# Forget gates, softmax scaling and the end of the first projection: three moves in a two-layer encoder kernel

## The chip, the cores and the metric

The kernel runs on one core of one Trainium2 chip. The metric is device time in microseconds of one execution, the median of the runs shown. One further execution was taken with the hardware profiler; all rows quoted here are from its profile and trace.

The engines are PE (TensorE, matmul), DVE (VectorE), ACT (ScalarE), POOL (GpSimd) and SP (SyncE, which issues most of the DMAs). Each takes its instructions from a queue, in order, so an instruction that waits holds up all that stand behind it on the same engine.

## The reference, cut to what matters

A sequence of 512 tokens of width 1024 goes through two layers. Each layer is a half-step SwiGLU, a mixer, and another half-step SwiGLU, each behind an RMSNorm with shift and scale. The change lies in the mixer:

```python
def hybrid_mixer(h, w_in, ...):
    proj = h @ w_in
    qa, ka, va, ub, qc, kc, vc, f_lin, g_lin = jnp.split(proj, SPLIT_POINTS, axis=-1)
    ya = chunked_relpos_attention(ha(qa), ha(ka), ha(va), ...)       # 8 heads of 64, learned bias
    yb = multiscale_pool(ub, w_pool, pool_scale)
    yc = forgetting_attention(hc(qc), hc(kc), hc(vc), ..., f_lin + forget_bias)
    ...
def forgetting_attention(q, k, v, gq, gk, f_logit):
    cum_logf = jnp.cumsum(jax.nn.log_sigmoid(f_logit), axis=1)       # per head, over the sequence
    logits = q k^T + (cq[..., None] - cum_k[:, :, None, :])          # causal
    p = jax.nn.softmax(logits, axis=-1)
    return p @ v
```

Queries and keys are RMS-normalised per head. Attention A is banded with a learned bias, attention C is causal with the forget gates as bias. The three branches are then gated, summed and projected.

## The kernel before

**Arithmetic.** Every large matmul is done as three passes of float32r: high part by high part, high by low, low by high (`triple`, line 117). A weight chunk is loaded by SP into a `raw` buffer (two of them), cast to its high part on ACT (line 268) and subtracted to its low part on DVE (line 270), by `wchunk`. `qkv_chunk` loads two of the eight 128-row blocks of one of the six 512-column projections.

**Order.** The code is unrolled Python, and a scheduler puts the instructions of each engine in order when the kernel is built, by the order in the code and by when it reckons operands to be ready. The code steers with a counter, `pe[0]`, in units of one 512-column pass on PE: a `triple` adds 3. `later(delay, fn)` sets a task due so many passes on; `poll`, called at each `triple`, runs what is due. `gate` and `behind` (lines 231 to 241) tie the weight casts and subtractions that follow a norm behind that norm's last instruction on ACT and DVE.

**The mixer** (`Mixer.run`, line 953):

1. `drain` runs the query, key and value projection of attention A one after the other (`proj_qk` with column block 0 and 1, `proj_v` with 2). A projection holds four accumulators (PSUM tag `acc`, four banks), one for each 128 tokens; `evac` empties them. For a query or key the evacuation is a copy and a square on ACT (lines 651 and 653) and a reduction on DVE (line 654); later tasks work out the norm, scale, and turn the result by transposes on PE (lines 660 to 694).
2. `attention` (line 777) goes through 8 heads of 4 row blocks. Row block i has (i + 1) x 128 columns. `logits` does two matmuls (lines 788, 789), bias and row maximum on DVE (792), Exp with row sum on ACT (796), the reciprocal on DVE (798) and the scaling of the row by it on POOL (799), and asks for `turn` `LAG_T` = 24 passes later. `turn` transposes the row on PE (811) and splits it in two parts on ACT and DVE (815, 816); `weigh`, `LAG_V` = 14 passes later, multiplies with the values (833, 834) and adds the halves (837 to 840). Between row blocks the loop draws products from a `filler` until the counter has gone up by a budget.
3. Attention A's filler is query, key and value projection of attention C and then `forget`, with a budget of `FILL_A` = 9.5. Attention C's filler is the merge of branch A (`merge_units`), with `FILL_C` = 9.0.

`forget` (line 726) does 16 matmuls of 40 output rows by 512 columns into a bank of the PSUM tag `mm`, then a chain of small instructions on 8 partitions: sums on DVE (740, 742), Exp on ACT (743), an addition (744), Ln on ACT (745), a difference (746), the running sum (748), and four differences (754); two DMAs write the result to memory, from where attention C's `strip_c` reads it back, spread over all partitions, as bias of each head. It is the last thing that the filler gives.

**The first projection** is special. Its first three weight chunks were loaded and split before the mixer (`self.pre`; the first two lie in the two buffers of tag `ptb`, one of which the evacuated query needs too), and the norm of the hidden state comes in two halves of 256 tokens. So `proj` (line 594) does six of the eight blocks for the first two token tiles, while the norm of the second half is made on DVE and ACT, then six blocks for the last two tiles. Only then is the fourth chunk asked for, and the last two blocks of all four tiles follow, each tile with its evacuation.

Working tiles that matter: `t1` has two buffers (biased logits, partial outputs), `t2` three (the scaled rows of the softmax from Exp to turn, and the squares of an evacuation).

Of the kernel before, what the change touches and what calls it, by code (L numbers as in the profile page):

```python
# [19 lines left out]
ALU = mybir.AluOpType  # L20
# [11 lines left out]
NT = T // P  # L32
# [8 lines left out]
def encoder_kernel(tc, xT, c, w_ada, b_ada, gains, w_gate, w_up, w_down, w_qkv, w_f, w_ubg,  # L41
                   qk_gain, rel, fbias, w_pool, pool_scale, w_branch, w_out, inv_cnt, w_first, out):
    nc = tc.nc
# [20 lines left out]
    def st(shape, dt, tag, bufs):  # L64
        return sb.tile(shape, dt, tag=tag, bufs=bufs, name=nm(tag))

    def acc(shape=(P, T)):
        return ps.tile(list(shape), F32, tag="acc", bufs=4, name=nm("acc"))

    def mmt(shape=(P, T)):  # L70
        return ps.tile(list(shape), F32, tag="mm", bufs=4, name=nm("mm"))
# [5 lines left out]
    def t1(cols=T):  # L77
        return st([P, cols], F32, "t1", 2)

    def t2(cols=T):  # L80
        return st([P, cols], F32, "t2", 3)
# [16 lines left out]
    def later(delay, fn, group=None):  # L98
        t = Task(pe[0] + delay, fn, group)
        tasks.append(t)  # L100
        return t
# [272 lines left out]
    def split_to(hi, lo, src):  # L374
        nc.scalar.copy(hi, src)
        nc.vector.tensor_tensor(lo, src, hi.bitcast(F32), op=ALU.subtract)
# [213 lines left out]
    def qkv_chunk(l, col, c, **kw):  # L590
        return wchunk(w_qkv[l, 2 * c * P:(2 * c + 2) * P, col * T:(col + 1) * T]
                      .rearrange("(k p) c -> p k c", p=P), (2, T), **kw)

    def proj(l, col, evac, pre=None, norm=None):
        accs = [acc() for _ in range(NT)]

        def three(t, k, hi, lo):
            tk = slice(t * P, (t + 1) * P)
            triple2(accs[t], hhi[:, k, tk], hlo[:, k, tk], hi, lo, k == 0, k == KD - 1)

        if norm is not None:
            for hs in range(2):
                norm.back(hs, mmt)
                if hs == 0:
                    later(FRONT2, lambda: norm.front(1, mmt))
                    later(BACK2, lambda: norm.back(1, mmt))
                for k in range(6):
                    hi, lo = pre[k // 2]
                    for t in (2 * hs, 2 * hs + 1):
                        three(t, k, hi[:, k % 2, :], lo[:, k % 2, :])  # L610
        else:
            for c in range(2):
                hi, lo = qkv_chunk(l, col, c)
                for kk in range(2):
                    for t in range(NT):
                        three(t, 2 * c + kk, hi[:, kk, :], lo[:, kk, :])
                        yield
        held = [(c, *qkv_chunk(l, col, c)) for c in ((3,) if pre else (2, 3))]
        for t in range(NT):
            for c, hi, lo in held:  # L620
                for kk in range(2):
                    three(t, 2 * c + kk, hi[:, kk, :], lo[:, kk, :])
                    yield
            evac(t, accs[t])

    def triple2(o, lh, ll, rh, rl, start, stop):
        triple(o, lh, ll, rh, rl, start, stop)

    def proj_v(l, col, tag, res):
        vt = [None] * NT  # L630

        def evac(t, a):
            b = st([P, H, 2, HD], F32R, tag, 4)
            a3 = a.rearrange("p (h d) -> p h d", h=H)
            for odd in range(2):
                hi, lo = b[:, odd::2, odd, :], b[:, odd::2, 1 - odd, :]
                split_to(hi, lo, a3[:, odd::2, :])
            vt[t] = b

        yield from proj(l, col, evac)  # L640
        res.extend(vt)
# [135 lines left out]
    def attention(qs, ks, vs, strip, ys, filler, budget, group):  # L777


        open_pt = {}  # L780

        def logits(h, i, strips):
            p, off = divmod(h, 2)
            (q, ql), k = qs[p], ks[p]
            odd = h % 2
            n = (i + 1) * P
            s = mmt()
            mm(s[:, :n], q[:, odd, i * P:(i + 1) * P], k[:, odd, :n], start=True, stop=False)
            mm(s[:, :n], ql[:, odd, i * P:(i + 1) * P], k[:, odd, :n], start=False, stop=True)
            lg = t1(T)[:, :n]  # L790
            mx = st([P, 1], F32, "mx", 4)
            nc.vector.tensor_tensor_reduce(out=lg, in0=s[:, :n], in1=strips[i], scale=-1.0, scalar=BIG,
                                           op0=ALU.add, op1=ALU.min, accum_out=mx)
            pr = t2(T)[:, :n]
            sm = st([P, 1], F32, "sm", 4)
            nc.scalar.activation(pr, lg, AF.Exp, bias=mx, scale=-1.0, accum_out=sm)  # L796
            rs = st([P, 1], F32, "rs", 4)
            nc.vector.reciprocal(rs, sm)  # L798
            nc.gpsimd.tensor_scalar(pr, pr, rs, None, op0=ALU.mult)  # L799
            pe[0] += 0.5 * (i + 1.5)  # L800
            later(LAG_T, lambda: turn(h, i, pr), group)

        def turn(h, i, pr):
            half, c = divmod(i, 2)
            nj = 2 * half + 2
            if c == 0:
                open_pt[h] = st([P, 2, nj, 256], F32R, "ptb" if half else "pta", 2 if half else 1)
            pt = open_pt[h]
            tp = mmt()
            for j in range(i + 1):  # L810
                nc.tensor.transpose(tp[:, j * P:(j + 1) * P], pr[:, j * P:(j + 1) * P], ident)  # L811
            tv = tp[:, :(i + 1) * P].rearrange("p (j q) -> p j q", q=P)
            dh = pt[:, 0, :i + 1, c * P:(c + 1) * P]
            dl = pt[:, 1, :i + 1, c * P:(c + 1) * P]
            nc.scalar.copy(dh, tv)
            nc.vector.tensor_tensor(dl, tv, dh.bitcast(F32), op=ALU.subtract)
            pe[0] += 0.55 * (i + 1)
            if c == 1:
                later(LAG_V, lambda: weigh(h, half, pt), group)

        def weigh(h, half, pt):
            p, off = divmod(h, 2)
            rows = slice(off * HD, off * HD + HD)
            other = slice(HD - off * HD, 2 * HD - off * HD)
            if off == 0 and half == 0:
                ys.append(blk("b"))
            y = ys[p]
            o = mmt((P, HALF))
            nj = 2 * half + 2
            for j in range(nj):  # L830
                q0 = P if j == nj - 1 else 0
                v2 = vs[j][:, h, :, :].rearrange("p a d -> p (a d)")
                mm(o[:, q0:], v2, pt[:, 0, j, q0:], start=(j == 0), stop=False)
                mm(o[:, q0:], v2, pt[:, 1, j, q0:], start=False, stop=(j == nj - 1))
            cols = slice(half * HALF, (half + 1) * HALF)
            yl = t1(T)[:, :HALF]
            nc.scalar.copy(yl[rows, :], o[other, :])
            nc.vector.tensor_tensor(yl[rows, :], o[rows, :], yl[rows, :], op=ALU.add)
            nc.scalar.copy(y[rows, 0, cols], yl[rows, :])
            nc.gpsimd.tensor_tensor(y[rows, 1, cols], yl[rows, :], y[rows, 0, cols].bitcast(F32), op=ALU.subtract)  # L840
            pe[0] += 1.0 * nj

        for h in range(H):
            strips = strip(h)
            if group == "c":
                finish_turns(h // 2)
            for i in range(NT):
                logits(h, i, strips)
                if i == NT - 1:
                    heads[0] = h + 1  # L850
                poll()
                goal = pe[0] + budget
                while filler is not None and pe[0] < goal:
                    if next(filler, "end") == "end":
                        filler = None
                poll()
        if filler is not None:
            for _ in filler:
                pass

    LAG_T, LAG_V = 24, 14


    def pool_front(l, g):
# [77 lines left out]
    class Mixer:  # L942
# [10 lines left out]
        def run(self, nxt):  # L953
            l = self.l
            in_ffn[0] = False
            for b in range(4):
                nc.gpsimd.dma_start(x_dram[b], x_blocks[b].rearrange("p a t -> p (a t)"))
            g = qkgc[:, l, :]
            g8 = qg8[:, l, :]
            qa, ka, va, qc, kc, vc = [], [], [], [], [], []  # L960
            ya, yb, yc = [], [], []
            drain(proj_qk(l, 0, g8[:, 0:1], True, qa, self.pre, self.norm),
                  proj_qk(l, 1, g[:, 1:2], False, ka), proj_v(l, 2, "xv", va))
            finish_turns()
            turns.clear()
            heads[0] = 0
# [1 line left out]
            def fill_a():  # L968
                yield from proj_qk(l, 3, g8[:, 2:3], True, qc)
                yield from proj_qk(l, 4, g[:, 3:4], False, kc)  # L970
                yield from proj_v(l, 5, "v2", vc)
                yield from forget(l)

            lo_share[0] = LO_SHARE
            attention(qa, ka, va, lambda h: strip_a(l, h), ya, fill_a(), FILL_A, "a")
# [61 lines left out]
                    d = c0 // P + j  # L1037
                    residual_tail(d, hs, o, modc[:, l, 5, d:d + 1], nxt)

    FILL_A, FILL_C = 9.5, 9.0  # L1040
    LO_SHARE = 0

    phases = []
# [65 lines left out]
```

## Time and profile before

| | |
|---|---|
| median of 3 runs | 2469.67 us (2468.43 to 2471.49) |
| the profiled execution | 2469.75 us |
| its span, first to last instruction | 2467.7 us |
| granted TensorE clock | 0.999 |
| POOL scaling of a row (line 799), all widths | 128 times, 138.4 us |

A page of the profile lists each engine's busy time. A row of the waits gives who waited for whom, the time in total, how often, and the longest. A row of the stages gives the stretch, its length and then for PE, PEld (weight loads of PE), DVE, ACT and POOL the busy time with the number of instructions in brackets, then the granted clock, the DMA share and GB/s. A row of the timeline gives start and duration in us, engine, line, operation, output and inputs, shapes, how many neighbours were merged, and in brackets the idle time before it and what ended it. A matmul is drawn longer than it holds PE: the next one of a run starts before its end.

### The profile page before, as it was taken

Reading aid. Unit: us, or ns where it says so; the run is one execution under the profiler, and the core shown is the slowest. Engines: PE = TensorE matmul, PEld = TensorE weight load, DVE = VectorE, ACT = ScalarE, POOL = GpSimd, SP = SyncE. Lnnn points to the kernel's source line nnn. Section 1 sums busy time; section 2 is a strip of 40 time slices with the busy share of each in tenths; the row PEclk is TensorE's granted clock in tenths of the full one; section 3 lists DMA queues with packets and bytes.
Section 4 is the critical chain, followed back from the end, with each engine's and each line's share of the span. In section 5 each row is a group of like instructions: output and inputs, shape, how many; then the busy total and the mean of one; then the engine's idle time right before and its main releaser. Section 6 shows DMA issues by size and latency. Waiting matters only on the chain.

```text
span 2467.7 us, 31105 instructions
## 1 busy us (share of the span) xinstructions
PE 2420.8 (98%) x11898; PEld 2027.6 (82%) x11898; DVE 1313.8 (53%) x2346; ACT 979.8 (40%) x1634; POOL 399.7 (16%) x455
## 2 busy tenths in 40 slices
PE   7999999998999999999999999999989999999999
PEld 5888888776888898888898888978778888888888
DVE  8655536676543465555365533376765434533332
ACT  5222235676632442223342222366765323422221
POOL 3000011145632200000100000112465322000000
PEclk9999999999999999999999999999999999999999
DMA  7655542223323435565335532323233233223222
GB/s 275 222 196 188 196 136 87 86 73 98 109 94 103 153 102 198 174 208 180 120 118 189 189 118 94 129 90 94 73 99 104 86 120 128 77 94 102 94 94 94
DMA packets 116264, 320.03 MB, mean 130 GB/s; under 512 B 11122, under 2 KB 13298, under 8 KB 116116
## 3 DMA queue, kind: packets, MB, share of 16 engines
q1 hardware_dynamic: 114962, 313.86, 38.3%
q0 software_dynamic: 1152, 4.19, 0.4%
q8 instruction: 93, 1.52, 0.3%
q14 instruction: 55, 0.45, 0.1%
q10 hardware_dynamic: 2, 0.00, 0.0%
HBM read 311.64 MB, written 6.38 MB: 129 GB/s over the span
## 4 chain that ended last, share of the span: by engine, by line
PE 86%; DVE 5%; ACT 5%; POOL 2%; issue 2%; DMA 0%; DVEq 0%; POOLq 0%; ACTq 0%
PE acc L119 14%; PE acc L120 14%; PE acc L121 14%; PE mm L121 14%; PE mm L119 14%; PE mm L120 14%; POOL t L799 1%; PE mm L811 1%; ACT whi L268 1%; ACT b L686 1%; DVE wlo L270 1%; ACT b L689 1%; DVE v L197 1%; POOL b L840 1%; ACT t L796 1%
## 5 line engine op out<-in xcount | busy, mean ns | idle before, releaser
L268 ACT CAST whi<-raw 128x1024 fp32r<-128x1024 f32 (+1 forms) x395 | 411.7, 1045 | 1076.5 <-PE acc L120 411.2
L270 DVE TENSOR_TENSOR wlo<-raw,whi 128x1024 fp32r<-128x1024 f32 x387 | 475.7, 1231 | 532.7 <-ACT whi L268 520.3
L121 PE MATMUL mm<-hhi,wlo 128*128 128x512 f32 x1304 | 507.5, 389 | 0.4 <-DVE wlo L270 0.4
L119 PE MATMUL mm<-hhi,whi 128*128 128x512 f32 x1304 | 507.7, 389 | 0.0
L120 PE MATMUL mm<-hlo,whi 128*128 128x512 f32 x1304 | 507.4, 389 | 0.0
L119 PE MATMUL acc<-b,whi 128*128 128x512 f32 (+1 forms) x960 | 356.0, 371 | 0.0
L120 PE MATMUL acc<-b,whi 128*128 128x512 f32 (+1 forms) x960 | 353.7, 368 | 1.3 <-POOL b L840 1.3
L121 PE MATMUL acc<-b,wlo 128*128 128x512 f32 (+1 forms) x960 | 354.0, 369 | 0.0
L121 PEld LDWEIGHTS mm<-hhi,wlo 128*128 128x128 f32 x1304 | 244.8, 188 | 51.5 <-DVE wlo L270 0.9
L119 PEld LDWEIGHTS mm<-hhi,whi 128*128 128x128 f32 x1304 | 245.1, 188 | 50.8
L120 PEld LDWEIGHTS mm<-hlo,whi 128*128 128x128 f32 x1304 | 244.8, 188 | 50.9
L197 DVE CUSTOM_DVE_ANT_0 v<-v,b,badac 128x1024 f32<-128x1024 f32 x144 | 189.3, 1316 | 34.5 <-DMA v<-in_w_ada_dram 34.4
L120 PEld LDWEIGHTS acc<-b,whi 128*128 128x128 f32 x960 | 181.2, 189 | 30.8 <-POOL b L840 1.9
L121 PEld LDWEIGHTS acc<-b,wlo 128*128 128x128 f32 x960 | 181.1, 189 | 29.8
L119 PEld LDWEIGHTS acc<-b,whi 128*128 128x128 f32 x960 | 181.1, 189 | 28.9
L119 PE MATMUL acc<-hhi,whi 128*128 128x512 f32 x480 | 190.8, 399 | 1.7 <-ACT hhi L563 1.7
L120 PE MATMUL acc<-hlo,whi 128*128 128x512 f32 x480 | 188.3, 392 | 1.1 <-DVE hlo L566 1.1
L121 PE MATMUL acc<-hhi,wlo 128*128 128x512 f32 x480 | 188.0, 392 | 0.0
L799 POOL TENSOR_SCALAR t<-t,rs 128x128 f32<-128x128 f32 (+3 forms) x128 | 138.4, 1084 | 251.1 <-DVE rs L798 220.3
L461 DVE TENSOR_TENSOR t<-mm,t 128x512 f32<-128x512 f32 x86 | 59.4, 691 | 204.7 <-PE mm L121 203.5
L119 PE MATMUL acc<-whi,hhi 128*128 128x512 f32 x336 | 137.9, 411 | 4.0 <-ACT t L653 3.6
L121 PE MATMUL acc<-whi,hlo 128*128 128x512 f32 x336 | 132.1, 393 | 0.0
(232 smaller groups left out, 3346.6 us busy)
## 6 DMA issues: line engine op xcount, KB each, us to landing
v<-in_w_ada_dram SPq DMA_DIRECT2D x144, 512.0 KB, 4.5
raw<-in_w_down_dram SPq DMA_DIRECT2D x88, 512.0 KB, 3.7
raw<-in_w_up_dram SPq DMA_DIRECT2D x82, 512.0 KB, 3.5
raw<-in_w_gate_dram SPq DMA_DIRECT2D x79, 512.0 KB, 3.6
raw<-in_w_ubg_dram SPq DMA_DIRECT2D x56, 512.0 KB, 3.5
raw<-in_w_qkv_dram SPq DMA_DIRECT2D x42, 512.0 KB, 3.8
raw<-in_w_branch_dram SPq DMA_DIRECT2D x24, 512.0 KB, 3.7
raw<-in_w_out_dram SPq DMA_DIRECT2D x16, 512.0 KB, 3.6
```

The lines of the kernel that those rows point to most:

```text
L119: mm(o, lh, rh, start=start, stop=False)
L120: mm(o, lh, rl, start=False, stop=False)
L121: mm(o, ll, rh, start=False, stop=stop)
L197: dot = nc.vector.tensor_tensor_reduce(out=raw, in0=raw, in1=silc[0], scale=1.0, scalar=badac[:, l, j, d:d + 1], op0=ALU.mult, op1=ALU.add ...
L268: nc.scalar.copy(hi, raw)
L270: lo_eng.tensor_tensor(lo, raw, hi.bitcast(F32), op=ALU.subtract)
L461: nc.vector.tensor_tensor(pr, pu, sg, op=ALU.mult)
L686: nc.scalar.activation(dst[own, :], pt[own, :], AF.Identity, scale=gc)
L689: nc.scalar.activation(low, pt[own, :], AF.Identity, scale=gc)
L796: nc.scalar.activation(pr, lg, AF.Exp, bias=mx, scale=-1.0, accum_out=sm)
L799: nc.gpsimd.tensor_scalar(pr, pr, rs, None, op0=ALU.mult)
L811: nc.tensor.transpose(tp[:, j * P:(j + 1) * P], pr[:, j * P:(j + 1) * P], ident)
```

## The change

It has four parts. In `proj`, when a norm is passed, the fourth chunk is asked for as soon as the first half's six blocks are issued, and the last two blocks and the evacuation follow for each half by itself. In `logits`, rows of 512 columns are scaled on VectorE, the others on GpSimd as before. The turn of a row is asked for 30 passes after its logits, in both attentions. `forget` moves from the end of attention A's filler to between the key and the value projection of attention A, and the filler's budget goes from 9.5 to 9.0.

```diff
@@ proj
+                both = (2 * hs, 2 * hs + 1)
                 for k in range(6):
                     hi, lo = pre[k // 2]
-                    for t in (2 * hs, 2 * hs + 1):
+                    for t in both:
                         three(t, k, hi[:, k % 2, :], lo[:, k % 2, :])
+                if hs == 0:
+                    rest = qkv_chunk(l, col, 3)
+                for t in both:
+                    for kk in range(2):
+                        three(t, 6 + kk, rest[0][:, kk, :], rest[1][:, kk, :])
+                    evac(t, accs[t])
+                yield
+            return
         else:
...
-        held = [(c, *qkv_chunk(l, col, c)) for c in ((3,) if pre else (2, 3))]
+        held = [(c, *qkv_chunk(l, col, c)) for c in (2, 3)]
@@ logits
-            nc.gpsimd.tensor_scalar(pr, pr, rs, None, op0=ALU.mult)
+            eng = nc.vector if i == NT - 1 else nc.gpsimd
+            eng.tensor_scalar(pr, pr, rs, None, op0=ALU.mult)
@@
-    LAG_T, LAG_V = 24, 14
+    LAG_T, LAG_V = 30, 14
@@ Mixer.run
             drain(proj_qk(l, 0, g8[:, 0:1], True, qa, self.pre, self.norm),
-                  proj_qk(l, 1, g[:, 1:2], False, ka), proj_v(l, 2, "xv", va))
+                  proj_qk(l, 1, g[:, 1:2], False, ka), forget(l),
+                  proj_v(l, 2, "xv", va))
...
                 yield from proj_v(l, 5, "v2", vc)
-                yield from forget(l)
@@
-    FILL_A, FILL_C = 9.5, 9.0
+    FILL_A, FILL_C = 9.0, 9.0
```

## The prediction

> **What bounds the kernel now.** I read the page first, then who waited for whom on PE, then the busy time of the engines stage by stage, and last the timeline around the few places that were left.
>
> ```profile
> span 2467.7 us, 31105 instructions
> ...
> PE 2420.8 (98%) x11898; PEld 2027.6 (82%) x11898; DVE 1313.8 (53%) x2346; ACT 979.8 (40%) x1634; POOL 399.7 (16%) x455
> ```
>
> TensorE is the bound: 46.9 us of the span are not matmul time. No edit removes a matmul, so all that can move is PE's waiting. The waits of PE, over the whole run:
>
> ```profile
> PE mm L811 <- POOL t L799: 13.2, 18, 1.8
> PE mm L552 <- ACT ssum L548: 4.6, 1, 4.6
> PE mm L539 <- DVE ssum L535: 4.0, 1, 4.0
> PE mm L145 <- ACT b L133: 3.7, 1, 3.7
> PE acc L119 <- ACT t L653: 3.6, 6, 1.3
> PE mm L788 <- DVE mx L792: 3.2, 6, 1.1
> PE mm L788 <- DVE t L838: 3.1, 5, 1.1
> ```
>
> L145, L539 and L552 belong to the start, which the change does not touch. The rest belongs to the mixer: the softmax transposes (L811) wait for the scaling on POOL (L799), projections wait for a bank that is still being evacuated (L653), logits (L788) wait for DVE. By stage, the first layer's mixer and one stage of the second's:
>
> ```profile
> 0.00:33.00 33.00, 19.01 (x56) 12.23 (x57) 25.41 (x45) 18.19 (x29) 10.21 (x12) 1.00 0.81 291
> ...
> 412.00:460.00 48.00, 46.73 (x222) 38.12 (x221) 34.58 (x64) 30.68 (x46) 0.00 (x0) 1.00 0.28 86
> 460.00:560.00 100.00, 95.51 (x500) 77.55 (x500) 72.45 (x187) 71.64 (x158) 42.05 (x50) 1.00 0.25 77
> 560.00:620.00 60.00, 52.37 (x280) 40.37 (x279) 39.92 (x111) 41.22 (x97) 37.98 (x50) 1.00 0.34 109
> 620.00:690.00 70.00, 69.17 (x371) 57.95 (x370) 40.37 (x104) 41.13 (x95) 40.44 (x50) 1.00 0.35 109
> ...
> 1780.00:1840.00 60.00, 52.74 (x278) 41.24 (x276) 39.77 (x110) 40.40 (x95) 37.63 (x49) 0.97 0.35 109
> ```
>
> The first figure after the length is PE's busy time. Idle: 1.3 in the key and value projection, 4.5 in attention A, 7.6 where A turns into C, 0.8 in the steady part of C, 14.2 us in all. The second layer repeats it (7.3 against 7.6 in the costly stage), so both layers hold about 28 us. That is the purse, and over half of it lies in 60 us at the A to C seam.
>
> **The change part by part.** *Forget gates between key and value.* The 16 matmuls are moved, not added. What they cover is this wait on PE:
>
> ```profile
> 435.90 0.39 PE L120 MATMUL acc<-wlo,hhi 128*128 128x512 f32 x1
> 436.13 0.39 PE L121 MATMUL acc<-whi,hlo 128*128 128x512 f32 x1
> 437.79 0.50 PE L119 MATMUL acc<-whi,hhi 128*128 128x512 f32 x1 [1.27 <-ACT t L653]
> ```
>
> Matmuls of 512 columns start every 0.23 us here; the value projection starts 1.66 us after the last one, so the wait costs 1.43, not the 1.27 called idle (0.16 more each time PE stops, since a matmul's end is drawn long). Sixteen matmuls at 0.23 are 3.7 us that need no accumulation bank, so the wait goes: -1.4 per layer, **-2.9** in all.
>
> At their old place the gates' vector steps stand in the queues of attention A:
>
> ```profile
> 565.01 0.73 DVE L740 SCALAR_TENSOR_TENSOR t<-mm,fbc,t 8x512 f32<-8x512 f32 x1
> ...
> 571.85 0.47 DVE L754 TENSOR_SCALAR ssum<-t 8x512 f32<-8x512 f32 x1
> ```
> ```profile
> 572.77 0.50 PE L788 MATMUL mm<-b,b 128*128 128x512 f32 x1 [1.05 <-DVE t L838]
> ...
> 575.28 0.33 PE L788 MATMUL mm<-b,b 128*128 128x128 f32 x1 [1.09 <-DVE mx L792]
> ```
>
> From 565.0 to 572.3 DVE works almost only for the gates, and directly behind them PE stops twice, for an attention output (L838) and a row maximum (L792) that stood in the queue. With 0.16 each that is 2.5 per layer, **-4.9**. At the new place the same 7.3 us of chain run beside the value projection (32 products of three matmuls, 22 us of PE). Queued behind it on DVE are the subtractions that make the value weights' low parts and the key's turning; ACT's table loads for Exp and Ln lie inside the chain; on SP the write of the gate vectors waits for its end, with weight loads behind it; the gates' own load and POOL's memset have nobody waiting. Cover is 3.7 us of new PE work, so the price lies between 0 and 7.3 - 3.7 = 3.6 per layer. The stage waits 1.3 today and DVE is busy 34.6 of 48, so I stay near the low end: 1 per layer, **+2**.
>
> *The pacing of attention A.* Without the gates the filler of A is 3 x 32 products of 3 passes, 288, which is 32 rows at 9.0; before it was 304, 32 rows at 9.5. But a budget of 9.5 is overrun: products come in threes, so a row takes 12 with little turning in it. Following the counter row by row through the code, the old filler is used up at the logits of row 7,0 and the last four rows are issued 6, 1, 1 and 2 passes apart; with 9.0 and no lump of 16 the filler lasts to the last row, which all stand 10 to 19 passes apart. The trace shows the bunch:
>
> ```profile
> 565.15 0.33 PE L788 MATMUL mm<-b,b 128*128 128x128 f32 x1 [0.25 <-DVE mx L792]
> 565.80 0.39 PE L788 MATMUL mm<-b,b 128*128 128x256 f32 x1
> 567.06 0.36 PE L788 MATMUL mm<-b,b 128*128 128x384 f32 x1
> ...
> 586.37 0.91 PE L811 MATMUL mm<-ident,t 128*128 128x128 f32 x5 [1.78 <-POOL t L799]
> ```
>
> Three rows' logits within 2 us, then PE at the transposes of the bunch, 1.78 in one stop.
>
> *Lag 30 and the scaling.* A lag of 24 passes is 5.6 us at 0.23, and the trace has it, rounded up to whole products, in steady C (this row's logits and its turn):
>
> ```profile
> 617.77 0.28 PE L788 MATMUL mm<-b,b 128*128 128x256 f32 x1
> ...
> 624.00 0.38 PE L811 MATMUL mm<-ident,t 128*128 128x128 f32 x2
> ```
>
> 6.2 us. Six more passes give every row 1.4 us more before PE asks for it. Rows of 512 columns also change engine:
>
> ```profile
> L799 POOL TENSOR_SCALAR t<-t,rs 128x512 f32<-128x512 f32 x32 | 50.1, 1566 | 42.6 <-DVE rs L798 30.1 <-DVE mx L792 3.7 <-PE mm L834 3.1
> L744 DVE TENSOR_SCALAR t<-t x2: 415/417/419, 567.2 to 1787.2; 8x512 f32<-8x512 f32 x2
> ```
>
> 1.57 us on POOL against 0.42 for the same operation and width on DVE: 1.15 sooner, and POOL is free for the next row. The trace has no such scaling over 128 partitions; its width per partition is the same, so I take 0.42, with the 0.73 of L740 as the upper end. It adds 32 x 0.42 = 13 us to DVE over four attentions, which cost nothing while DVE has room (72 of 100 in A, 40 of 70 in C); without that room they would push each row's chain by 0.42, which the 1.4 covers. The longest L811 stop is 1.8, so lag alone covers most of the 18. They cost 13.2 + 18 x 0.16 = 16.1; bounds are 0 (the stops move on) and -16.1. I take three quarters, **-12**. What is left in the two layers, 28 - 2.5 - 4.3 - 13.2 = 8 us, is mostly of the seam too; I take half, **-4**.
>
> One thing speaks against the new engine, in three rows:
>
> ```profile
> 412.66 0.18 DVE L662 TENSOR_SCALAR nt_v<-qss 128x32 f32<-128x32 f32 x1
> ```
> ```profile
> 530.53 2.14 POOL L799 TENSOR_SCALAR t<-t,rs 128x256 f32<-128x256 f32 x2 [3.14 <-DVE rs L798]
> ```
> ```profile
> 531.51 0.53 DVE L662 TENSOR_SCALAR nt_v<-qss 128x32 f32<-128x32 f32 x1
> ```
>
> The same DVE operation takes 0.18 with POOL idle and 0.53 while POOL is scaling. So a scaling on DVE that meets a busy POOL (some 40 of 100 us) may take the rest of one POOL scaling more, at worst 1.1, half of the 2.14 of the two; at 0.42 + 1.1 a row of 512 would gain nothing over POOL's 1.57, and the 35 us for all 32 would be DVE's, 9 per attention. That would take some 4 us of the 12 and give 2457. The Trainium skill (SBUF — State Buffer, "Who interferes with whom") says that a VectorE tensor_scalar in its two-port mode and a GpSimd instruction shut each other out for the whole of an instruction; the rows above fit it, and by it the sum would be that 2457, without it 2453. I keep 2453, since POOL gives up its longest scalings with the same edit.
>
> The price of the longer lag: a row holds one of three t2 buffers 1.4 us longer, and the squares of the evacuations want one too. By the counter a head of C is 53.5 passes, so three rows are 40, 9.2 us; from logits to the end of the turn a row takes 6.6 above (617.77 to 624.38) and then 8.0, and it holds the buffer for less than that. It fits, with an evacuation in A sometimes late: between 0 and the 1.4 of the K to V wait at each of two seams, I take 1.5 per layer, **+3**.
>
> *First projection half by half.* Today it has almost no wait. What matters is when the last chunk's weights exist:
>
> ```profile
> 396.73 0.51 PE L119 MATMUL acc<-ptb,hhi 128*128 128x512 f32 x1
> ```
> ```profile
> 401.37 1.99 ACT L268 CAST whi<-raw 128x1024 fp32r<-128x1024 f32 x2
> ```
> ```profile
> 402.44 2.36 DVE L270 TENSOR_TENSOR wlo<-raw,whi 128x1024 fp32r<-128x1024 f32 x2 [0.46 <-ACT whi L268]
> ```
>
> Cast and subtraction are tied behind the second half's norm pieces and end at 402.4 and 403.6; the second half's products start at 396.73. Nothing can be gained, since there is no wait to remove; two evacuations come a little earlier, and not before the second half has used the first chunk, whose ptb buffer they need. It costs from 0 (the second half's products go first) to 403.6 - 396.7 = 6.9 per layer (PE stands at the last chunk). I take 1, **+2**.
>
> Sum: -2.9 - 4.9 + 2 - 12 - 4 + 3 + 2 = -16.8. The profiled execution took 2469.75, 2.05 beyond its span, and stands 0.08 over the median of 2469.67. Forecast: 2453.
>
> **The rivals.** *PE stands in the first projection (slower).* If the last chunk's products stand in PE's queue ahead of the second half's, PE waits 6.9 per layer, +13.8; with only the two certain gains (-7.8) and the small prices of gates and buffers (+5) that is +11: 2481. It decides as soon as these twelve matmuls stand first, and the other gains stay under 11. Against it: PE's order follows readiness elsewhere, since merge products fill in between rows of attention that the code issues earlier. For it: the code now issues them first.
>
> *The stops move on (no change).* Orders in all queues are made anew; if transposes wait for DVE where they waited for POOL, the 12 and 4 are not had: -7.8 + 7 = -1, 2469. For it: DVE is the busier engine. Against it: steady C, with evenly spaced rows, has 0.8 in 70 us.
>
> *The lag does nothing or the scaling is shut out (less gain).* Then only even pacing and the gates' move work: -7.8 - 8 + 5 = -11, 2459. Against: lag 24 shows as 6.2 us.
>
> *All stops go (more gain).* -2.9 - 4.9 - 16.1 - 8 and no new wait: -32, 2438. For it: steady C is nearly there already.
>
> **How the numbers follow.** Forecast (2446 to 2457) 0.50; less gain 0.18; more gain 0.13; the stops move on 0.10; PE stands in the first projection 0.09. A measurement of this kernel tells 0.2%, 4.9 us, from no change. Three cases lie faster by more: 0.81; same 0.10; slower 0.09. The range takes the forecast, most of more gain and all of less gain, to 2438 below, and half of no change, to 2467 above.
>
> **What would show it.** Right: the K to V wait is gone; the L788 waits behind the gates are gone and the gates' scan runs beside the value projection; the A to C stage (60 us) has under 3 us of PE idle; L811 on POOL falls from 13.2 to under 4; scaling of 128x512 on DVE takes about 0.42. Wrong: a PE wait for L268 or L270 some 10 us into the first projection; L811 waiting for DVE; more than 4 us of idle in the value projection.

## The result and the profile after

The changed kernel takes 2453.53 us (median of 6 runs, 2451.83 to 2454.71) against 2471.38 (6 runs, 2468.43 to 2473.49): 17.9 us less, a ratio of 0.9927 with a 95% interval of 0.9916 to 0.9937. The forecast was 2453. The profiled execution took 2454.57.

The page after, span and engines. Line numbers from 607 on have moved: L797 is the logits' matmul (788 before), L801 the row maximum (792), L805 Exp (796), L809 the scaling (799), L821 the row's transposes (811), L686 the transposes of queries and keys (677), L850 the subtraction of an output's low half on POOL (840).

```profile
span 2452.8 us, 31079 instructions
...
PE 2415.4 (98%) x11898; PEld 2028.4 (83%) x11898; DVE 1325.7 (54%) x2378; ACT 976.6 (40%) x1634; POOL 343.1 (14%) x423
```

The same matmuls, 5.4 us less of drawn PE time and 9.5 us less idle (37.4 for 46.9). What PE waited for, after the three waits of the start:

```profile
PE mm L821 <- DVE t L809: 4.0, 4, 1.5
PE mm L686 <- DVE ptb L826: 2.4, 2, 1.2
PE acc L119 <- ACT whi L268: 2.1, 2, 1.2
PE mm L821 <- DVE t L848: 1.9, 2, 1.0
PE mm L686 <- DVE ptb L681: 1.7, 4, 0.6
```

The 18 stops of the transposes for POOL are gone; four for the scaling on DVE have come, and a tail of small ones. The stops for the weight cast (L268) lie at the seams (571.57 in the first layer), not in the first projection, where the prediction had looked for one. Where the time went is read by stage. I cut the first layer's mixer into four, by its own first logits in each attention: the 48 us ahead of attention A's first logits; attention A; the seam, from 14 us before C's first logits to 26 after; and 84 us of C. Before, then after:

```profile
412.00:460.00 48.00, 46.73 (x222) 38.12 (x221) 34.58 (x64) 30.68 (x46) 0.00 (x0) 1.00 0.28 86
460.00:561.00 101.00, 96.51 (x506) 78.18 (x506) 73.19 (x189) 72.41 (x160) 42.30 (x51) 1.00 0.25 77
561.00:601.00 40.00, 33.93 (x179) 25.13 (x178) 27.06 (x73) 27.45 (x64) 22.16 (x31) 1.00 0.34 110
601.00:685.00 84.00, 81.61 (x445) 68.42 (x444) 49.72 (x134) 51.72 (x125) 54.37 (x67) 1.00 0.36 112
```
```profile
416.00:464.00 48.00, 47.13 (x222) 37.33 (x221) 36.62 (x66) 33.41 (x50) 0.75 (x3) 1.00 0.31 95
464.00:556.00 92.00, 87.51 (x468) 71.42 (x467) 70.88 (x189) 69.93 (x154) 34.89 (x46) 1.00 0.27 81
556.00:596.00 40.00, 39.12 (x215) 32.91 (x214) 28.24 (x76) 27.69 (x68) 20.06 (x29) 1.00 0.36 112
596.00:680.00 84.00, 81.97 (x444) 68.47 (x443) 52.51 (x140) 50.23 (x123) 35.56 (x57) 1.00 0.35 110
```

Length less PE's busy time: 1.27, 4.49, 6.07 and 2.39 us before; 0.87, 4.49, 0.88 and 2.03 after. The seam gives 5.2 of the 6.0 us of this layer; attention A up to the seam gives nothing. Stretches of one length need not hold the same work, so these figures say where PE stood; they do not add up to a run's time. The second layer, cut in the same way, gives 3.8 us (1.28, 4.45, 5.72 and 2.26 before; 0.87, 4.51, 1.42 and 3.10 after). Together that is 9.8, near the 9.5 of the whole run.

The spans differ by 14.9, so 5.4 us are drawn PE time. Some 17 stops fewer, at the prediction's 0.16 each, would make 2.7 of it; that is an estimate, and no run measures it alone. Another part goes with the granted clock. In the kernel before it was lower for a while behind a stop of 1.78 us in the second seam:

```profile
1806.42 1.23 PE L811 MATMUL mm<-ident,t 128*128 128x128 f32 x5 [1.78 <-POOL t L799]
```
```profile
1800.00:1810.00 10.00, 8.15 (x39) 6.17 (x37) 6.13 (x18) 6.35 (x17) 5.63 (x8) 0.83 0.10 31
```

The second seam of the changed kernel shows 1.00:

```profile
1767.00:1807.00 40.00, 38.58 (x211) 32.23 (x210) 28.58 (x77) 26.79 (x67) 18.96 (x28) 1.00 0.36 112
```

A clock of 0.83 over 10 us is 1.7 us of matmul time, an estimate. The executions point the same way: of 66 of the kernel before that were timed beside the experiments, the four with a granted clock of 1.000 took 2469.0 us on average, the ten with 0.997 took 2473.0 (one more, at 0.728, took 3110.49 and is left out); all six of the changed kernel had 1.000. Against the former the gain is 15.4 us, so some 2.4 of the 17.9 go with the clock. No run holds the clock fixed.

### The profile page after: what moved, and what is told of

It reads as the page before. It is cut to its first block, busy times and chain, and to the rows that moved or that the text cites. A ratio compares the mean times of both kernels' runs of the same rounds, so it can differ in the third digit from the quotient of the medians.

```text
span 2452.8 us, 31079 instructions
## 1 busy us (share of the span) xinstructions
PE 2415.4 (98%) x11898; PEld 2028.4 (83%) x11898; DVE 1325.7 (54%) x2378; ACT 976.6 (40%) x1634; POOL 343.1 (14%) x423
## 5 line engine op out<-in xcount | busy, mean ns | idle before, releaser
L268 ACT CAST whi<-raw 128x1024 fp32r<-128x1024 f32 (+1 forms) x395 | 411.9, 1046 | 1060.2 <-PE acc L120 403.5
L120 PE MATMUL acc<-wlo,hhi 128*128 128x512 f32 x336 | 131.6, 392 | 0.0
```

Source lines behind the costliest of these rows:

```text
L120: mm(o, lh, rl, start=False, stop=False)
L268: nc.scalar.copy(hi, raw)
```

## The experiments

Two theories stood at first. SEAM: the gain comes from the gates' chain leaving the queues where A turns into C, and from A's last rows being issued evenly. TURN: it comes from transposes that no longer meet an unscaled row, by lag and faster scaling. Twelve kernels were run; all figures are medians with the ratio to the kernel before on the same chip. Idle is PE's, in the four stages cut as above.

| run | us | ratio, 95% interval | idle: K and V, A, seam, C |
|---|---|---|---|
| kernel before | 2471.38 | | 1.27, 4.49, 6.07, 2.39 |
| changed | 2453.53 | 0.9927 (0.9916 to 0.9937) | 0.87, 4.49, 0.88, 2.03 |
| a1 gates only | 2465.83 | 0.9981 (0.9972 to 0.9990) | 0.87, 7.05, 0.53, 5.45 |
| a2 lag only | 2474.72 | 1.0017 (1.0009 to 1.0026) | 1.26, 5.53, 4.08, 3.41 |
| a3 scaling only | 2468.14 | 0.9988 (0.9980 to 0.9997) | 1.32, 4.84, 4.25, 2.20 |
| a4 first projection only | 2471.48 | 1.0003 (0.9994 to 1.0012) | 1.30, 4.54, 5.70, 2.20 |
| r1 all but gates | 2465.36 | 0.9979 (0.9970 to 0.9988) | 1.28, 4.52, 3.99, 3.26 |
| r2 all but lag | 2462.14 | 0.9970 (0.9958 to 0.9982) | 0.87, 7.30, 0.43, 3.00 |
| r3 all but scaling | 2457.86 | 0.9948 (0.9935 to 0.9960) | 0.87, 4.85, 1.21, 2.50 |
| r4 all but first projection | 2452.88 | 0.9928 (0.9916 to 0.9940) | 0.87, 4.50, 1.12, 2.00 |
| m2 gates, budget 9.5 | 2463.68 | 0.9973 (0.9963 to 0.9983) | 0.87, 4.30, 4.33, 2.06 |
| x3 lag, gates mid filler | 2468.49 | 0.9993 (0.9984 to 1.0001) | 1.30, 7.59, 0.19, 4.98 |
| x2 changed, lag 36 | 2444.50 | 0.9894 (0.9879 to 0.9909) | 0.87, 4.03, 0.65, 0.12 |
| x4 changed, low half on DVE | 2445.14 | 0.9897 (0.9883 to 0.9910) | 0.87, 4.01, 0.62, 0.12 |

**One part alone.** Gates moved, with the budget at 9.0:

```diff
-                  proj_qk(l, 1, g[:, 1:2], False, ka), proj_v(l, 2, "xv", va))
+                  proj_qk(l, 1, g[:, 1:2], False, ka), forget(l),
+                  proj_v(l, 2, "xv", va))
-                yield from forget(l)
-    FILL_A, FILL_C = 9.5, 9.0
+    FILL_A, FILL_C = 9.0, 9.0
```

> The kernel before with the gates moved between key and value and the filler's budget at 9.0, nothing else. Theory SEAM (the gain comes from the seam of attention A and C: the gates' chain leaves the queues and the last rows of A are issued evenly): -11 to -15 us, most of the 18 that the whole change brought, with PE idle in the A to C stage down from 7.6 to under 3 us per layer. Rival TURN (the gain comes from turns that no longer meet an unscaled row, by the longer lag and the faster scaling): -5 to -8 us, the two waits of the gates and the wait between key and value, and the stops of L811 on POOL stay near 13 us in all.

It gave 5.5, not 11 to 15. The seam did what SEAM said, 6.07 to 0.53, but A and C took most of it back: 4.49 to 7.05 and 2.39 to 5.45. In C the largest wait of ACT from 595 to 690 us of this run (its sum, its count, the longest; 6.4 us in the kernel before) points to a reason, and the timeline of POOL, ACT and PE shows one place:

```profile
ACT t L928 <- POOL b L840: 14.2, 7, 2.9
```
```profile
647.84 2.28 POOL L774 TENSOR_TENSOR strip<-strip,cmask 128x128 f32<-128x128 f32 x3 [1.25 <-DMA strip<-fv_dram]
650.08 0.73 POOL L840 TENSOR_TENSOR b<-t,b 64x256 fp32r<-64x256 f32 x1
```
```profile
650.85 0.60 ACT L928 ACTIVATE t<-acc 128x512 f32<-128x512 f32 x1 [2.64 <-POOL b L840]
651.34 0.71 ACT L796 ACTIVATE t<-t,mx 128x512 f32<-128x512 f32 x1
```
```profile
654.14 0.66 PE L811 MATMUL mm<-ident,t 128*128 128x128 f32 x4 [0.74 <-POOL t L799]
```

The merge's tanh (L928) needs one of two t1 buffers. One is held by an attention output until POOL has subtracted its low half (L840), and that stands behind three mask additions. ACT stands 2.64 us at the head of its queue, and the Exp of a 512-column row, whose maximum had been ready, stands behind it. Six microseconds of lag are then too few, and PE stops at the transposes. I had followed rows and engines, and not this buffer. No run took this wait away at a lag of 24, so how much of C's 5.45 it makes is argued, not shown.

The lag alone:

```diff
-    LAG_T, LAG_V = 24, 14
+    LAG_T, LAG_V = 30, 14
```

> The kernel before with the lag at 30 passes, nothing else. SEAM: -3 to -7 us, since by the counter the longer lag alone also keeps A's last rows apart (12 to 26 passes instead of 1 or 2), while the gates' chain stays where it was. TURN: -10 to -13 us, the stops of L811 on POOL nearly gone.

It lost 3.4 us; both theories expected a gain. The stops at POOL's scaling, which TURN expected nearly gone, still cost 11.0 of 13.2 us, in 8 stops instead of 18. With the longer lag the rows of A go through the filler evenly, as the counter had it, and the gates come out at the very end of A. The timeline across the seam:

```profile
578.46 0.28 SPq L756 DMA_DIRECT2D fv_dram<-ssum  x1
...
583.60 1.29 POOL L774 TENSOR_TENSOR strip<-strip,cmask 128x128 f32<-128x128 f32 x3 [3.36 <-DMA strip<-fv_dram]
...
584.09 0.29 DVE L792 CUSTOM_DVE_ANT_0 t<-mm,strip 128x128 f32<-128x128 f32 x1 [2.87 <-POOL strip L774]
```

The gates are written at 578.5, are back as C's bias at 583.6, and the first row maximum of C follows at 584.1. Its logits had been issued at 568.7. The table does not show this loss, since its last stretch ends before this run's C does. From the first logits of C to its last product with the values it takes 116.9 us, against 107.0 in the kernel before, while A is only 6.6 us shorter.

Scaling on VectorE alone, and the first projection alone (their lines as in the change):

```diff
-            nc.gpsimd.tensor_scalar(pr, pr, rs, None, op0=ALU.mult)
+            eng = nc.vector if i == NT - 1 else nc.gpsimd
+            eng.tensor_scalar(pr, pr, rs, None, op0=ALU.mult)
```

> The kernel before with rows of 512 columns scaled on VectorE, nothing else. SEAM: within 3 us of before. TURN: -4 to -7 us, the stops of L811 on POOL down by the third or more that stand at rows of 512 columns. If VectorE and GpSimd shut each other out, scalings on VectorE that take over 1 us show it.

3.1 us less, between the two. Stops at POOL's scaling fell from 13.2 to 5.3 us, so TURN's mechanism was there, and most of its gain was not. The longest scaling on DVE took 0.78 us, under the 1 us that would have shown the engines shutting each other out at length.

> The kernel before with the first projection ended half by half, nothing else. Both theories: within 2 us of before. The rival that PE stands at the last chunk in the first projection: +5 to +14 us and a PE wait for L268 or L270 there.

0.2 us slower, as expected, and no PE wait for the last chunk.

**All but one.** Each undoes one of the diffs above in the changed kernel.

> The changed kernel with the gates back at the end of A's filler and the budget back at 9.5; lag 30, scaling on VectorE and the halved first projection stay. SEAM: it keeps little of the gain, -3 to -7 us against the kernel before, since the gates' chain is back in the queues at the seam; PE idle in the A to C stage over 4 us per layer. TURN: it keeps -10 to -13 us.

> The changed kernel with the lag back at 24 passes. SEAM: within 4 us of the changed kernel, so -14 to -18 us against the kernel before. TURN: it loses 6 us or more, -12 us or less against the kernel before, and L821 waits for L809 again.

> The changed kernel with all rows scaled on GpSimd again. SEAM: within 3 us of the changed kernel. TURN: it loses 4 us or more, at transposes of rows of 512 columns that wait for L809 on POOL.

Without the gates' move 4.8 us of gain are left (against 2470.13 on that chip), without the lag 8.0, without the scaling 12.3. So in company the gates are worth 13, the lag 10 and the scaling 6, while alone they gave 5.5, lost 3.4 and gave 3.1. Neither theory stands by itself: r1 fell as SEAM said, r2 and r3 lost more than SEAM allowed, as TURN said. In r2 PE waits for POOL's scaling again (6.5 us), and the ACT waits for L850 are 30.3 us over the whole run, as in a1 (30.6); the kernel before has 12.9. In the changed kernel they are 2.1, and DVE waits for L850 instead, 20.9.

> The changed kernel with the first projection as before. BOTH and ORDER alike: within 2 us of the changed kernel, as the halved projection alone was 0.2 us from the kernel before. If the halved projection matters in company of the other parts, 4 us or more away.

17.8 us under the kernel before on that chip, as the changed kernel was on its own: it does not matter in company either.

**Pacing against the gates' chain.** Gates moved as in a1, the budget left at 9.5:

> The kernel before with the gates moved between key and value but the budget left at 9.5, lag 24, scaling on GpSimd. By the counter the filler, now 288 passes, is used up at the fourth row of head 6 and the last five rows of attention A are issued 1 to 5 passes apart, as in the kernel before, but without the gates' chain. It splits SEAM in two: if even pacing carries the gain of the seam, it is slower than the run with budget 9.0 by 5 us or more and PE idles over 5 us per layer where A turns into C; if the gates' chain carries it, the two are within 3 us.

Its seam, PE's logits of 128 to 512 columns by start and duration:

```profile
563.25 0.39 PE L788 MATMUL mm<-b,b 128*128 128x512 f32 x1
563.70 0.22 PE L788 MATMUL mm<-b,b 128*128 128x128 f32 x1
564.49 0.39 PE L788 MATMUL mm<-b,b 128*128 128x256 f32 x1
565.94 0.44 PE L788 MATMUL mm<-b,b 128*128 128x384 f32 x1 [0.26 <-DVE mx L792]
566.63 0.41 PE L788 MATMUL mm<-b,b 128*128 128x512 f32 x1
```

Five rows are issued within 3.4 us, and there are 4.33 us of idle in the seam against 0.53 with 9.0. Even pacing carries most of the seam, then, and the chain of the gates the rest (6.07 to 4.33). But the run as a whole was not 5 us slower than a1: against its own kernel before it gained 6.5 us, a1 5.5, and C idles 2.06 instead of 5.45. The total did not follow the stage that I had meant to test.

**Lag without the late gates.** The second pair of theories: BOTH (lag loses only where it makes the gates late) and ORDER (every new order moves stops about).

```diff
                 yield from proj_qk(l, 4, g[:, 3:4], False, kc)
+                yield from forget(l)
                 yield from proj_v(l, 5, "v2", vc)
-                yield from forget(l)
```

> The kernel before with lag 30 and the gates earlier in attention A's filler, between key and value projection of attention C; budget 9.5, scaling on GpSimd, first projection as before. Theory BOTH (lag 30 alone loses because it puts the gates' chain and its trip through memory right before attention C's first row, which needs them; away from there the longer lag gains): the cost of C's first two heads falls from 9 us per layer to under 4 and the run is 6 to 12 us under the kernel before, against +4 with the lag alone. Rival ORDER (any new order moves stops about by some 5 us, and lag 30 is no gain without the other parts): within 4 us of the kernel before.

The seam fell to 0.19, so the late gates were what held it in a2. The total moved by 2.2 us only, since A rose to 7.59 and C to 4.98: the 6 to 12 that BOTH expected were a miss, and the total is where ORDER put it. Why A rises here was not settled. In a1 and r2 it rises by the same stops (1.14 and 1.01 us at 520.1, 0.86 and 0.85 at 524.7, 1.94 and 1.95 at 530.8); both have a lag of 24 with a budget of 9.0.

**What limits the changed kernel.** Two edits of it: `LAG_T` 36, and one engine in `weigh`:

```diff
-            nc.gpsimd.tensor_tensor(y[rows, 1, cols], yl[rows, :], y[rows, 0, cols].bitcast(F32), op=ALU.subtract)
+            nc.vector.tensor_tensor(y[rows, 1, cols], yl[rows, :], y[rows, 0, cols].bitcast(F32), op=ALU.subtract)
```

> The changed kernel with the lag at 36 passes. If lag only gives slack and slack is still short at some rows: 1 to 4 us under the changed kernel. If the three t2 buffers bind, as the prediction priced for lag 30 (rows of A stand as near as 31 passes for three): 3 to 10 us over the changed kernel, with Exp, and the evacuations' squares, waiting for transposes.

> The changed kernel with the low half of an attention output subtracted on VectorE instead of GpSimd (64 times 64x256, 0.73 us on GpSimd when free, about 0.4 on VectorE). If the stops that are left in attention C come from the t1 buffer that this subtraction holds while logits wait for it (maximum of a 512-column row waiting for L850): 2 to 6 us under the changed kernel. If VectorE's queue has become the limit: 2 us or more over it.

In the changed kernel's C the last long stop is this one, by the timelines of POOL, DVE and PE:

```profile
669.02 0.73 POOL L850 TENSOR_TENSOR b<-t,b 64x256 fp32r<-64x256 f32 x1 [2.08 <-ACT b L849]
```
```profile
669.78 0.69 DVE L801 CUSTOM_DVE_ANT_0 t<-mm,ssum 128x512 f32<-128x512 f32 x1 [0.95 <-POOL b L850]
```
```profile
673.29 0.63 PE L821 MATMUL mm<-ident,t 128*128 128x128 f32 x4 [1.52 <-DVE t L809]
```

The maximum of a 512-column row waits for t1, which an attention output holds until POOL's subtraction is done; here that had itself waited for ACT's copy (L849). The maximum comes 4.1 us after its logits (669.78 after 665.72), in x4 2.9 us after them (665.65 after 662.74). With the subtraction on DVE (0.45 us each) the maxima wait 0.5 us for it in all, its 29 us on DVE cost nothing that can be seen, and C idles 0.12. Below are x4's stretch of C and its subtraction's group. That shortens the hold on t1 without touching pacing or lag, and the run is 8.4 us under the changed kernel. It also takes 64 instructions out of POOL's queue; no run separates the two. Lag 36 gets the same C by outwaiting it (waits of DVE for L850 fall from 20.9 to 7.5 us). Both gains are larger than expected (8.4 for 2 to 6, and 9.0 for 1 to 4). Together the two edits were not run.

```profile
594.00:678.00 84.00, 83.88 (x455) 70.75 (x454) 60.35 (x155) 51.00 (x122) 28.64 (x45) 1.00 0.35 113
```
```profile
L850 DVE TENSOR_TENSOR b<-t,b 64x256 fp32r<-64x256 f32 x64 | 29.1, 454 | 5.2 <-ACT b L849 3.2
```

## Why the prediction was right, and where it was not

*The sum and the place.* Forecast -16.8, measured -17.9; the purse of 28 us, over half of it at the seam, was read rightly, and the seam fell below the 3 us that the forecast named. That the sum came within 1.1 us is partly luck: two prices that were charged (+3 and +2) did not come, the 2.4 us that go with the clock had no term, nor had the stops behind t1, which still cost 8.4 in the changed kernel.

*Gates between key and value: right, as a net.* Forecast -2.9 and +2. The wait of 1.27 is gone, but the stage still idles 0.87: the chain stands ahead of the key's scaling on DVE, and the key's transposes wait, the price that was named. DVE and PE in the changed kernel:

```profile
444.15 0.74 DVE L749 SCALAR_TENSOR_TENSOR t<-mm,fbc,t 8x512 f32<-8x512 f32 x1
```
```profile
446.19 1.89 DVE L681 TENSOR_TENSOR ptb<-ptb,nt_z 128x512 f32<-128x512 f32 x3
```
```profile
449.07 0.33 PE L686 MATMUL mm<-ident,ptb 128*128 128x128 f32 x1 [0.60 <-DVE ptb L681]
```

*Gates' chain and pacing: right.* a1 and m2 show both in the seam. There the chain is worth 1.7 us of drawn idle time a layer (6.07 to 4.33), where its two stops had been put at 2.1; the pacing is worth 3.8 (4.33 to 0.53).

*Lag and scaling, -12 and -4: the stops went, but not by these parts alone.* Stops at the scaling fell from 13.2 to 4.0, close to "under 4". The step "lag alone covers most of the 18" failed: with the lag alone 11.0 of the 13.2 us stayed. But A, where I put part of it, idles 4.49 as before: other stops came. The forecast took the parts as independent prices. Alone they add up to -5.5 + 3.4 - 3.1 + 0.2 = -5, together they make -17.9. Neither -12 nor -4 has a measured size of its own. Without late gates the lag gained 2.2 us (x3) instead of losing 3.4, with the gates moved and A paced evenly 10. Even pacing with a lag of 24 (a1, r2) meets waits of 30 us on ACT for t1, which in the changed kernel are 2.1 (and 20.9 on DVE); that these waits are what the lag pays for is the likeliest reading. That buffer was in no term.

*Buffers, +3: wrong.* The three t2 buffers hardly bind: ACT waits for a transpose to free one 1.1 us in all at 30 and 3.0 at 36, and 36 is 9 us faster.

*First projection, +2 and the slower rival: wrong, it is nothing.* a4 and r4 lie within 0.2 us. PE's order puts the last chunk's products in among those of the second half, and no wait for them shows.

*Scaling on DVE: 0.49 us, not 0.42; being shut out by POOL almost never happens,* since POOL rarely scales when a 512-column row is due: in 28 of 32 cases it took 0.48 to 0.49, and the longest 0.73. The 2457 of the sum with shutting out did not come.

## What to carry to other kernels

In a kernel where PE is 98% busy, price a change by the stages that still idle, and look there for a wait at the head of a queue: ACT waiting for a buffer that POOL frees delayed an Exp that needed neither. Delay, pacing and a moved chain are not additive; a longer delay alone was a loss here, and 10 us of gain in company. Before a delay is priced as too long for its buffers, try it longer.

## What the runs showed of the hardware

VectorE and GpSimd lengthened each other's instructions. In the changed kernel a scaling on DVE took 0.73 instead of 0.49 in the two cases where POOL had begun to clear a tile (four clearings in a row below); in four cases where a clearing began after it, it took 0.48:

```profile
514.02 0.73 DVE L809 TENSOR_SCALAR t<-t,rs 128x512 f32<-128x512 f32 x1
```
```profile
513.95 2.38 POOL L699 MEMSET b<- 64x512 f32 x4
```

And in a1 the three mask additions on POOL took 2.28 (above) beside a DVE subtraction with two SBUF inputs, where the kernel before has them at 1.29:

```profile
647.98 1.40 DVE L270 TENSOR_TENSOR wlo<-raw,whi 128x1024 fp32r<-128x1024 f32 x1
```
```profile
602.26 1.29 POOL L774 TENSOR_TENSOR strip<-strip,cmask 128x128 f32<-128x128 f32 x3 [0.51 <-DMA strip<-fv_dram]
```

Behind another of these subtractions a scaling of 128 columns on POOL took 1.58 us in a1, against 0.59 to 0.61 in the kernel before. The subtraction that holds t1 is lengthened too, from 0.73 to as much as 2.02 us in the kernel before:

```profile
654.13 1.46 DVE L270 TENSOR_TENSOR wlo<-raw,whi 128x1024 fp32r<-128x1024 f32 x1 [0.35 <-ACT whi L268]
```
```profile
654.48 1.58 POOL L799 TENSOR_SCALAR t<-t,rs 128x128 f32<-128x128 f32 x1
```

The Trainium skill (SBUF — State Buffer, "Who interferes with whom") says that a VectorE instruction in a two-port mode, which a tensor_scalar can enter, and GpSimd shut each other out for a whole instruction, with the one that issues first going on, and that a VectorE instruction with two SBUF inputs contends with GpSimd's reads. The rows above agree, 0.73 for 0.49 and 1.58 for 0.60; no run here separates the lock from another cause.
